# Entering the feed-forward of a hybrid mLSTM and attention block: first weights by seven products, weight sums by adding loads

## The chip, the cores and the metric

The kernel runs on one core of one Trainium2 chip. The metric is device time in microseconds. The kernel before took 1544.88 us (median of three runs, 1544.74 to 1545.6).

Engines are named as in the profile: PE is TensorE (matrix products), DVE is VectorE, ACT is ScalarE, POOL is GpSimd, SP is the engine that issues most transfers.

## The reference

One layer over 1024 tokens of width 1024, everything in float32. An mLSTM mixer and a sparse-attention mixer give two branches; gated, they are summed to `mixed`. What matters for the change is what follows:

```python
h = h + mixed @ w_out                      # 1024 x 1024
f = rms_norm(h, g_norm_ffn)                # per token
h = h + (silu(f @ w_gate) * (f @ w_up)) @ w_down   # 1024 -> 2816 -> 1024
return rms_norm(h, g_final)
```

## The kernel before, in words

**Numbers.** Each float32 operand is split into a rounded high part and a low part (`split_steps`, L1867: a copy on ScalarE, a subtraction on VectorE). A product of two operands is three matmuls (`mm3`, L353 to L355): high times high, high times low, low times high. The word "product" below stands for 12 matmuls of 128 x 128 by 512: four slices of the inner dimension, three matmuls each.

**Seven products for eight.** The products with `w_out`, with the gate and up weights and with `w_down` use a scheme of Winograd's kind. Operands are cut 2 x 2: inner dimension in two halves of 512, rows in even and odd blocks of 128 tokens, columns in two halves. Instead of eight block products there are seven, of sums of blocks; they are numbered by `q`, 1 to 7. Operand 1 and 2 of the rows are the two halves of the even rows; 3 to 7 involve the odd rows too.

**w_out.** For every `q` there are four products, one for each pair of row blocks `j` (`wprod`, L2058). Their results are combined (`post`, L2084) in the buffers `xp[r, c, j]` (r: even or odd row block, c: column half). The input `x` is added by a transfer from memory that adds into the buffer (`xadd`, L2078, through `dma_add`, L1874, issued on GpSimd). Weight sums of `w_out` are made by such adding loads too (`wo_add`, L1991, 1 MB each).

**Passage to the feed-forward.** A finished row half is stored and its squares are summed (`stored`, L2147, `square`, L2096). From two halves the norm factor follows (`rstd_steps`, L2100). `rows_f` (L2153) scales the row (`stt`, L2120: for all even and half the odd rows on ScalarE and then GpSimd, else on VectorE), transposes it on TensorE (L2166, four transposes to a tile), and `row0` (L2173) or `row1` (L2181) and `row1_rest` (L2194) split it or its sums into the operands `fsb[q, j]`.

**Feed-forward.** There are 22 weights `m`: even `m` are gate blocks, odd `m` up blocks, of 256 columns each. The first two, `m` = 0 and 1, are multiplied plainly (`plain_ops`, L2201, `plain`, L2211): four result blocks, two halves of the inner dimension, so eight products each, the four blocks of the even rows first; for the odd rows an extra operand `q` = 8 is made. The other 20 weights go by seven products in the order 1, 2, 6, 7, 5, 4, 3 (`seq`). `load_raw` (L2251) loads a weight in two 512 KB pieces. `sums` (L2259) makes four weight sums: one by a load and an adding load, three on VectorE. `prep` (L2286) splits an operand into one of six operand slots (`OSLOT`), `product` (L2322) multiplies and adds to what was kept, and `finish` (L2302) applies SiLU or multiplies by the gate and stores a tile to `d_gu`.

**The order.** The code lists steps in program order. `Plan` (L66) then places them on the engines by a model of their durations: each engine's queue takes, among the first 60 to 140 steps listed for it (PE: 60), the one that can start first, ties by rank. `pl.boost` raises the rank of the steps listed under it. The result is one fixed order for each engine, GpSimd's and SP's transfers included. A step waits on the chip for what it reads and for its buffer. [...]

Of the kernel before, what the change touches and what calls it, by code (L numbers as in the profile page):

```python
# [9 lines left out]
F32R = mybir.dt.float32r  # L10
# [162 lines left out]
def body(ctx, tc, a, out):  # L173
# [1904 lines left out]
    def xadd(r, c, j):  # L2078
        b = xp[r, c, j]
        i = 2 * j + r  # L2080
        src = a["x"][P * i:P * i + P, 512 * c:512 * c + 512]
        dma_add(lambda: b.ap, lambda: src, [b], 6000.0)
# [70 lines left out]
    def rows_f(r, j):  # L2153
# [27 lines left out]
    def row1(j):  # L2181
        p12, p22 = rows_f(1, j)
        c11, c21 = xp[0, 0, j], xp[0, 1, j]
        at = lambda b: (lambda: four(b.ap))
        t1, t2, t7 = (fpiece((3 * j + n) // 2, (3 * j + n) % 2) for n in range(3)) if j < 2 else (xp[1, 0, j], xp[1, 1, j], fpiece(3, j % 2))
        tsum[j] = {5: t1, 6: t2, 7: t7, 4: c21}
        fsplit(8, j, at(p12), [p12])
        fsplit(3, j, at(p22), [p22])
        act(587.0, lambda: t7.ap, lambda: p12.ap, AF.Copy, [p12], [t7])
        into(V, t1, p12, c11, ALU.subtract, [p12, c11])  # L2190
        into(V, t2, p22, t1, ALU.subtract, [p22, t1])
        into(V, t7, p22, t7, ALU.subtract, [p22])

    def row1_rest(q):  # L2194
        for j in range(4):
            b = tsum[j][q]
            if q == 4:
                into(V, b, b, tsum[j][6], ALU.subtract, [tsum[j][6]])
            fsplit(q, j, lambda b=b: four(b.ap), [b])

    def plain_ops(m):  # L2201
        for kh in range(2):
            b = slot_buf(28 + kh)
            src = a["w_up" if m else "w_gate"].rearrange("(k p) c -> p k c", p=P)
            dma(lambda b=b: rows4(b), lambda kh=kh, src=src: src[:, 4 * kh:4 * kh + 4, 0:256], (), [b])
            for h in range(2):
                o = OB[m, kh, h] = slot_buf(((31, 33, 32, 34), (6, 7, 4, 5))[m][2 * h + kh], F32R)
                src_ = lambda b=b, h=h: rows4(b)[:, :, P * h:P * h + P]
                split_steps(lambda o=o: four(o.ap[:, 0, :]), lambda o=o: four(o.ap[:, 1, :]), src_, [b], [o])

    def plain(m, r, c):  # L2211

        ps = pl.buf()
        fq = ((1, 2), (8, 3))[r]

        for kh in range(2):
            def go(e, kh=kh):
                o, (fh_, fl_) = OB[m, kh, c], blk(fq[kh])
                for k in range(4):
                    mm3(ps.ap, o.ap[:, 0, P * k:P * k + P], o.ap[:, 1, P * k:P * k + P], fh_[:, k], fl_[:, k], kh + k == 0, kh * k == 3)  # L2220
            pl.step((("PE", 12 * 226.7),), go, [OB[m, kh, c]] + [fsb[fq[kh], j] for j in range(4)], [ps])
        if m == 0:
            t = sil[0, (r, c)] = epiece(20 + 2 * c + r)
            act(587.0, lambda: t.ap, lambda: ps.ap, AF.Silu, [ps], [t])
            return
        t, g = epiece(11 + ncount["u"] % 3), sil[0, (r, c)]
        ncount["u"] += 1
        ew(V, lambda: t.ap, lambda: ps.ap, lambda: g.ap, ALU.mult, [ps, g], [t])
        dma(lambda: d_gu[c][:, 512 * r:512 * r + 512], lambda: t.ap, [t], [gub[c]])
# [5 lines left out]
    seq = [(m, q) for m in range(2, NM) for q in (1, 2, 6, 7, 5, 4, 3)]  # L2235
    LO, HI = slice(0, P), slice(P, 2 * P)
    RB, SB_, OB = {}, {}, {}
    EP = (20, 21, 11, 8, 12, 13, 22, 4, 2, 1, 23, 9, 7, 3, 5, 10, 6, 0)

    def epiece(n):  # L2240
        n = EP.index(n)
        return xpiece(n) if n < 16 else piece(60 + n - 16)

    RSLOT = (28, 29, 4, 5)
    OSLOT = (31, 33, 32, 34, 6, 7)
    gub = [pl.buf((), True) for _ in range(NFF)]

    def rows4(b):
        return b.ap.rearrange("p a (k c) -> p (a k) c", k=2)

    def load_raw(n):  # L2251
        m, z = divmod(n, 2)
        if m >= NM:
            return
        b = RB[m, z] = slot_buf(RSLOT[n % 4])
        src = a["w_up" if m % 2 else "w_gate"].rearrange("(k p) c -> p k c", p=P)
        dma(lambda: rows4(b), lambda: src[:, 4 * z:4 * z + 4, 256 * (m // 2):256 * (m // 2) + 256], (), [b], kb=512.0)

    def sums(m, n):  # L2259
        if (m, n) in SB_:  # L2260
            return SB_[m, n]
        r0, r1 = RB[m, 0], RB[m, 1]
        sub = lambda b, h: (lambda: rows4(b)[:, :, h])
        x, y, alu, rd = {1: (sub(r0, HI), sub(r1, HI), ALU.add, [r0, r1]),
                         2: (None, sub(r0, LO), ALU.subtract, [r0]),
                         3: (sub(r0, LO), sub(r0, HI), ALU.subtract, [r0]),
                         4: (sub(r1, LO), None, ALU.subtract, [r1])}[n]
        b = epiece({1: m % 2, 2: 2 + m % 2, 3: 4, 4: 4}[n])
        if n == 1:
            src = a["w_up" if m % 2 else "w_gate"].rearrange("(k p) c -> p k c", p=P)  # L2270
            part = lambda z: src[:, 4 * z:4 * z + 4, 256 * (m // 2) + P:256 * (m // 2) + 2 * P]
            dma(lambda: four(b.ap), lambda: part(0), (), [b])
            dma_add(lambda: four(b.ap), lambda: part(1), [b], 5500.0)
            SB_[m, n] = b
            return b
        if n in (2, 4):
            o = sums(m, n // 2)
            rd = rd + [o]
            x, y = (x or (lambda: four(o.ap))), (y or (lambda: four(o.ap)))
        ew(PREP, lambda: four(b.ap), x, y, alu, rd, [b])  # L2280
        SB_[m, n] = b
        return b

    nop = [0]

    def prep(m, q):  # L2286
        j = nop[0]
        nop[0] += 1
        if q in (1, 2, 4):
            r = RB[m, 0 if q == 1 else 1]  # L2290
            h = HI if q == 4 else LO
            src = lambda: rows4(r)[:, :, h]
        else:
            r = sums(m, {3: 4, 5: 1, 6: 2, 7: 3}[q])
            src = lambda: four(r.ap)
        b = OB[m, q] = slot_buf(OSLOT[j % 6], F32R)
        split_steps(lambda: four(b.ap[:, 0, :]), lambda: four(b.ap[:, 1, :]), src, [r], [b], PREP)

    keep, sil = {}, {}
    ncount = {"u": 0}  # L2300

    def finish(m, blk, ps, other):  # L2302

        s_, w = divmod(m, 2)
        r, c = blk
        if w:
            t = epiece(11 + ncount["u"] % 3)
            ncount["u"] += 1
        else:
            t = epiece(20 + 2 * r + c)  # L2310
# [11 lines left out]
    def product(m, q, part=None):  # L2322
# [11 lines left out]
        if part == 0:  # L2334
            return
# [351 lines left out]
```

## Time and profile before

| | |
|---|---|
| median of three runs | 1544.88 us |
| profiled execution | 1544.09 us |
| its span, first to last instruction | 1542.3 us |
| granted TensorE clock | 0.998 |
| w_out products with group q = 1, from | 809.72 us |
| last eight w_out products, from | 864.65 us |
| even rows of the first two weights | 894.61 to 920.98 us |

Times in a row of the timeline are microseconds from the span's start, then the length. A matmul's bar is longer than the distance to the next, as they are pipelined; the pace is read from starts. In a table of windows each engine has its busy time and number of instructions, then come the clock, the DMA engines' mean busy share and GB/s. A wait row names the waiting engine, what it waited for, total time, times, longest.

### The profile page before, as it was taken

Reading aid. Unit: us, or ns where it says so; the run is one execution under the profiler, and the core shown is the slowest. Engines: PE = TensorE matmul, PEld = TensorE weight load, DVE = VectorE, ACT = ScalarE, POOL = GpSimd, SP = SyncE. Lnnn points to the kernel's source line nnn. Section 1 sums busy time; section 2 is a strip of 40 time slices with the busy share of each in tenths; the row PEclk is TensorE's granted clock in tenths of the full one; section 3 lists DMA queues with packets and bytes.
Section 4 is the critical chain, followed back from the end, with each engine's and each line's share of the span. In section 5 each row is a group of like instructions: output and inputs, shape, how many; then the busy total and the mean of one; then the engine's idle time right before and its main releaser. Section 6 shows DMA issues by size and latency. Waiting matters only on the chain.

```text
span 1542.3 us, 22142 instructions
## 1 busy us (share of the span) xinstructions
PE 1507.2 (98%) x7618; PEld 1271.8 (82%) x7618; DVE 1130.6 (73%) x2393; ACT 807.6 (52%) x1715; POOL 225.0 (15%) x297
## 2 busy tenths in 40 slices
PE   6999999999999999999999999999999999999997
PEld 5877888887989889888888778888888888888886
DVE  6978888875988688875666786666666666785795
ACT  5325566652888688876425664333333333454453
POOL 2000000013121312210001420000000000423311
PEclk9999999999999999999999999999999999999999
DMA  8434755589151924129927724444544443998731
GB/s 278 122 76 119 239 163 164 163 235 281 41 121 41 176 51 115 40 48 342 261 92 177 171 75 116 111 110 126 155 114 110 111 111 106 261 288 179 154 94 55
DMA packets 198777, 223.40 MB, mean 145 GB/s; under 512 B 11960, under 2 KB 144470, under 8 KB 198664
## 3 DMA queue, kind: packets, MB, share of 16 engines
q1 hardware_dynamic: 158024, 175.72, 36.7%
q0 software_dynamic: 40352, 45.60, 18.8%
q8 instruction: 60, 0.98, 0.3%
q10 hardware_dynamic: 288, 0.66, 0.1%
q14 instruction: 53, 0.43, 0.1%
HBM read 171.51 MB, written 58.29 MB: 149 GB/s over the span
## 4 chain that ended last, share of the span: by engine, by line
PE 85%; DVE 6%; DMA 6%; ACT 2%; issue 1%; SPq 0%; DVEq 0%; ACTq 0%; POOLq 0%
PE PS L354 16%; PE PS L353 16%; PE PS L355 16%; PE bk L353 5%; PE bk L354 5%; PE bk L355 5%; PE T L1526 4%; PE obank L1548 2%; PE obank L1546 2%; PE d L353 2%; PE d L355 2%; PE d L354 2%; DMA UTL_float<-in_x 1%; DMA d_mg<-S 1%; DMA ra<-in_w_gate 1%
## 5 line engine op out<-in xcount | busy, mean ns | idle before, releaser
L1862 DVE TENSOR_TENSOR UTL_float<-PS,UTL_float 128x512 f32<-128x512 f32 x160 | 107.5, 688 | 85.2 <-PE PS L355 84.1
L1535 DVE TENSOR_TENSOR TL<-T,TH 128x512 fp32r<-128x512 f32 (+1 forms) x184 | 103.3, 582 | 28.7 <-ACT TH L1531 27.8
L1531 ACT ACTIVATE TH<-T 128x512 fp32r<-128x512 f32 (+1 forms) x184 | 90.3, 510 | 26.4 <-PE T L1526 23.1
L354 PE MATMUL PS<-quad_float32r,sl_float32r 128*128 128x512 f32 x216 | 84.0, 389 | 0.0
L353 PE MATMUL bk<-UTH,op 128*128 128x512 f32 x192 | 77.4, 403 | 0.0
L355 PE MATMUL bk<-UTH,op 128*128 128x512 f32 x192 | 75.0, 391 | 0.0
L354 PE MATMUL bk<-UTL,op 128*128 128x512 f32 x192 | 74.9, 390 | 0.0
L353 PE MATMUL PS<-quad_float32r 128*128 128x512 f32 x192 | 74.8, 390 | 0.0
L355 PE MATMUL PS<-quad_float32r 128*128 128x512 f32 x192 | 74.7, 389 | 0.0
L354 PE MATMUL PS<-quad_float32r 128*128 128x512 f32 x192 | 74.7, 389 | 0.0
L354 PE MATMUL PS<-quad_float32r,whi 128*128 128x512 f32 x168 | 65.5, 390 | 0.7 <-DVE quad_float32r L1862 0.7
L354 PE MATMUL PS<-quad_float32r,wh 128*128 128x512 f32 x164 | 63.8, 389 | 0.0
L353 PE MATMUL bk<-T,op 128*128 128x512 f32 x144 | 58.1, 404 | 0.0
L1560 POOL DMA_DIRECT2D d_yn<-os x32 | 31.9, 996 | 174.1 <-DMA d_yn<-os 40.7
L355 PE MATMUL bk<-T,op 128*128 128x512 f32 x144 | 56.3, 391 | 0.0
L354 PE MATMUL bk<-T,op 128*128 128x512 f32 x144 | 56.2, 390 | 0.0
L353 PE MATMUL d<-UTH,whi 128*128 128x512 f32 x128 | 53.0, 414 | 1.9 <-ACT mg L1398 1.7
L355 PE MATMUL d<-UTH,wlo 128*128 128x512 f32 x128 | 50.4, 394 | 0.0
L354 PE MATMUL d<-UTL,whi 128*128 128x512 f32 x128 | 50.3, 393 | 0.0
L353 PE MATMUL PS<-UTH_float32r,sl_float32r 128*128 128x512 f32 x124 | 48.4, 391 | 0.0
L355 PE MATMUL PS<-UTH_float32r,sl_float32r 128*128 128x512 f32 x124 | 48.3, 389 | 0.0
L725 ACT ACTIVATE op<-S 128x512 fp32r<-128x512 f32 x40 | 25.1, 629 | 43.6 <-PE bk L354 35.0
(1463 smaller groups left out, 4919.6 us busy)
## 6 DMA issues: line engine op xcount, KB each, us to landing
rp<-in_w_in SPq DMA_DIRECT2D x22, 512.0 KB, 4.5
d_gu<-UTL_float SPq DMA_DIRECT2D x44, 256.0 KB, 3.3
sl_float<-in_w_up SPq DMA_DIRECT2D x20, 512.0 KB, 3.8
quad_float<-d_mg SPq DMA_DIRECT2D x32, 256.0 KB, 6.5
d_rep<-d_row SPq DMA_DIRECT2D x8, 960.0 KB, 7.4
raw<-in_w_gate SPq DMA_DIRECT2D x11, 512.0 KB, 4.3
ra<-in_w_gate SPq DMA_DIRECT2D x11, 512.0 KB, 4.2
rp<-in_w_in SPq DMA_DIRECT2D x20, 256.0 KB, 5.0
```

What stands on the lines that cost most here:

```text
L353: nc.tensor.matmul(ps, ah, bh, start=first, stop=False)
L354: nc.tensor.matmul(ps, ah, bl, start=False, stop=False)
L355: nc.tensor.matmul(ps, al, bh, start=False, stop=last)
L725: step1("ACT", 525.0, lambda: nc.scalar.activation(h, src(), AF.Copy), [r], [b])
L1526: nc.tensor.transpose(pt[:, z, P * r:P * r + P], e, ident)
L1531: nc.scalar.activation(hl[0][:, 0:m], pt[:, 0:m], AF.Copy)
L1535: nc.vector.tensor_tensor(hl[1][:, 0:m], pt[:, 0:m], cast32(hl[0])[:, 0:m], ALU.subtract)
L1546: nc.tensor.matmul(po, vv, th[:, z, :], start=(st[1] == 0), stop=False)
L1548: nc.tensor.matmul(po, vv, tl[:, z, :], start=False, stop=(st[1] == st[2]))
L1560: low_half.append(lambda: nc.gpsimd.dma_start(dst, half(1), accum_op=ALU.add))
L1862: return pl.step(alts, lambda e: ENG[e].tensor_tensor(out_(), x(), y(), alu), reads, writes, **kw)
```

## The change

1. `m` = 0 and 1 go by seven products like the others. `plain_ops`, `plain` and operand 8 go. The even rows' products 1 and 2 of weights 0 to 3 come first; then weights 0 and 1 take turns in the order 7, 6, 3, 5, 4; then weights 2 and 3 take that order, one after the other; later weights take 1, 2, 7, 6, 3, 5, 4.
2. All weight sums are made by adding loads: four buffers of 256 KB for each weight, one of which (`x`) is loaded, added to, split for product 7, added to, split for 6, added to, split for 3. Signs are settled in `finish` (SiLU with a factor -1, a multiply with -1).
3. Rows are scaled on VectorE alone.
4. In w_out, the sum for `xp[0, 1]` is started as a copy of `xp[1, 1]` during group 5, and its `x` is added then, ahead of the last product; the adds for the odd rows wait until the 1 MB adding load of `w_out` behind group 3 has landed (`reads=[WT[1]]`). A tiny square root on ScalarE is put ahead of group 3's results. The last eight products run in the order 4, 4, row, 7, row, 7, 4, row, 4, row, 7, 7 instead of 7, row, 4 for each `j`.
5. Stored tiles of `d_gu` are tracked by half, and buffers are handed out from lists (`wfree`, `efree`); the list of free buffers of the down projection has another order.

```diff
-    def xadd(r, c, j):
+    def xadd(r, c, j, reads=()):
...
-            stt(lambda b=b: b.ap, lambda b=b: b.ap, i, lambda c=c: gFb.ap[:, c, :], [gFb], [b], r == 0 or j < 2)
+            stt(lambda b=b: b.ap, lambda b=b: b.ap, i, lambda c=c: gFb.ap[:, c, :], [gFb], [b])
...
     def row1(j):
         p12, p22 = rows_f(1, j)
...
-        fsplit(8, j, at(p12), [p12])
-        fsplit(3, j, at(p22), [p22])
-        act(587.0, lambda: t7.ap, lambda: p12.ap, AF.Copy, [p12], [t7])
-        into(V, t1, p12, c11, ALU.subtract, [p12, c11])
-        into(V, t2, p22, t1, ALU.subtract, [p22, t1])
-        into(V, t7, p22, t7, ALU.subtract, [p22])
+        c11, c21, t7, t6 = xp[0, 0, j], xp[0, 1, j], xp[1, 0, j], xp[1, 1, j]
+        tsum[j] = {7: t7, 6: t6, 5: c11, 4: c21}
+        into(V, t7, c11, p12, ALU.subtract, [p12, c11])
+        fsplit(7, j, lambda: four(t7.ap), [t7])
+        stt_neg(lambda: t6.ap, lambda: p22.ap, lambda: t7.ap, [p22, t7], [t6])
+        fsplit(3, j, lambda: four(p22.ap), [p22])
...
-    seq = [(m, q) for m in range(2, NM) for q in (1, 2, 6, 7, 5, 4, 3)]
+    seq = [(m, q) for q in (7, 6, 3, 5, 4) for m in (0, 1)] + [(m, q) for m in (2, 3) for q in (7, 6, 3, 5, 4)]
+    seq += [(m, q) for m in range(4, NM) for q in (1, 2, 7, 6, 3, 5, 4)]
     OSLOT = (31, 33, 32, 34, 6, 7)
...
+    def w_add(m, n, h, kh):
+        b = WA[m, n]
+        dma_add(lambda: four(b.ap), lambda: w_blk(m, h, kh), [b], 5500.0)
+
+    def prep(m, q):
+        t = {1: "y", 2: "b", 7: "x", 6: "x", 5: "y", 3: "x", 4: "d"}[q]
+        s = WA[m, t]
+        b = OB[m, q] = slot_buf(OSLOT[nop[0] % 6], F32R)
+        nop[0] += 1
+        split_steps(lambda: four(b.ap[:, 0, :]), lambda: four(b.ap[:, 1, :]), lambda: four(s.ap), [s], [b], PREP)
+        if q == 1:
+            w_add(m, "y", 1, 0)
+        elif q == 7:
+            w_add(m, "x", 0, 0)
+        elif q == 6:
+            w_add(m, "x", 0, 1)
+        else:
+            wfree.append(s.home)
+        if q == 3:
+            w_load(m, "d", 1, 1)
+        elif q == 2 and m > 3:
+            chain_load(m)
+
+    def chain_load(m):
+        w_load(m, "x", 1, 1)
+        w_add(m, "x", 1, 0)
...
         out_piece(1, 1, j)
         post(1, 1, j, b5[j], (1, 0), 3)
-        xadd(1, 0, j)
+        out_piece(0, 1, j)
+        act(587.0, lambda d=xp[0, 1, j]: d.ap, lambda x=xp[1, 1, j]: x.ap, AF.Copy, [xp[1, 1, j]], [xp[0, 1, j]])
+        xadd(0, 1, j)
     prep_ab(3, 1)
     wo_add(1, 0, 1)
+    for j in range(4):
+        xadd(1, 1, j, [WT[1]])
+        xadd(1, 0, j, [WT[1]])
+    pl.step((("ACT", 1500.0),), lambda e: nc.scalar.activation(warm, eps, AF.Sqrt), [xp[0, 1, 0]], ())
     b3 = bank()
     for j in range(4):
         wprod(3, j, b3[j])
-        out_piece(0, 1, j)
-        post(0, 1, j, b3[j], (1, 1), 2)
-        xadd(0, 1, j)
-        xadd(1, 1, j)
+        post(0, 1, j, b3[j], None, 2)
+        stored(0, 1, j)
...
     pl.boost = 80
-    for m in range(2):
-        for c in range(2):
-            plain(m, 0, c)
+    for m in range(4):
+        product(m, 1)
+        product(m, 2)
+        if m == 0:
+            for q in (1, 2):
+                prep(3, q)
+            for c in range(4):
+                chain_load(c)
     pl.boost = 0
...
     for n, (m, q) in enumerate(seq):
+        if n < 10 and m == 0 and q in (6, 5, 4):
+            row1_rest(q)
         prep(m, q)
         product(m, q)
+        if q == 3 and 3 <= m < NM - 1:
+            first_loads_e(m + 1)
```

More of the change, by code (lines that the diff above doesn't have):

```diff
@@ L2211, in plain @@
[L2211 to L2229, printed above, removed]
@@ L2251, in load_raw @@
-    def load_raw(n):
-        m, z = divmod(n, 2)
-        if m >= NM:
-            return
[L2255 to L2282, printed above, removed]
@@ L2320, in body @@
-    pb = {}
-    def product(m, q, part=None):
-        o = OB[m, q]
-        ps = pb.setdefault((m, q), pl.buf())
-        js = slice(0, 4) if part is None else slice(2 * part, 2 * part + 2)
-        cs = slice(P * js.start, P * js.stop)
+    seq = [(m, q) for q in (7, 6, 3, 5, 4) for m in (0, 1)] + [(m, q) for m in (2, 3) for q in (7, 6, 3, 5, 4)]
+    seq += [(m, q) for m in range(4, NM) for q in (1, 2, 7, 6, 3, 5, 4)]
+    OSLOT = (31, 33, 32, 34, 6, 7)
+    gub = {(t, c): pl.buf((), True) for t in range(NFF) for c in range(2)}
@@ new lines, in body, with wtake, etake, w_blk @@
+    wfree = [(n, z) for n in (28, 29, 4, 5) for z in range(2)]
+    efree = [(n, z) for n in (0, 1, 2, 3, 30) for z in range(2)]
+    WA, OB, nop = {}, {}, [0]
+    def wtake():
+        n, z = wfree.pop(0)
+        b = fpiece(n, z)
+        b.home = (n, z)
+        return b
+    def etake():
+        h = efree.pop(0)
+        b = xpiece(h[1]) if h[0] == "x" else fpiece(*h)
+        b.home = h
+        return b
+    def w_blk(m, h, kh):
+        src = a["w_up" if m % 2 else "w_gate"].rearrange("(k p) c -> p k c", p=P)
+        c0 = 256 * (m // 2) + P * h
+        return src[:, 4 * kh:4 * kh + 4, c0:c0 + P]
@@ new lines, in chain_load, with first_loads_e, finish @@
+    def chain_load(m):
+        w_load(m, "x", 1, 1)
+        w_add(m, "x", 1, 0)
+    def first_loads_e(m):
+        w_load(m, "y", 0, 0)
+        w_load(m, "b", 0, 1)
+    acc, sil = {}, {}
+    def finish(m, b, r, c, flip=False):
+        s_, w = divmod(m, 2)
+        if w == 0:
+            pl.step((("ACT", 520.0),), lambda e: nc.scalar.activation(b.ap, b.ap, AF.Silu, scale=-1.0 if flip else 1.0), (), [b])
+            sil[s_, r, c] = b
+            return
+        g = sil.pop((s_, r, c))
+        if flip:
+            pl.step((("DVE", 670.0),), lambda e: nc.vector.scalar_tensor_tensor(b.ap, b.ap, -1.0, g.ap, ALU.mult, ALU.mult), [g], [b])
+        else:
+            ew(PREP, lambda: b.ap, lambda: b.ap, lambda: g.ap, ALU.mult, [g], [b])
+        dma(lambda: d_gu[2 * s_ + r][:, 512 * c:512 * c + 512], lambda: b.ap, [b], [gub[2 * s_ + r, c]])
+        efree.extend(x.home for x in (g, b) if x.home[0] in ("x", 30))
@@ L2329, in go, with product @@
+    def product(m, q):
+        o = OB.pop((m, q))
+        ps = pl.buf()
         def go(e):
@@ L2422, in body @@
     wo_add(0, 1, 0)
-    plain_ops(0)
+    for m in range(2):
+        first_loads_e(m)
+        prep(m, 1)
+        prep(m, 2)
     b6 = bank()
@@ L2440, in body, with p4, p7 @@
         wprod(3, j, b3[j])
[L2441 to L2444 removed]
+        post(0, 1, j, b3[j], None, 2)
+        stored(0, 1, j)
     gFb = pl.buf(keys_of(30), make=lambda: f32(30))
     dma(lambda: flat(gFb.ap), lambda: a["g_norm_ffn"].partition_broadcast(P), (), [gFb], kb=512.0)
+    prep_ab(4, 0)
     prep_ab(7, 1)
[L2448 to L2455 removed]
+    b4, b7 = {}, {}
+    def p4(j):
+        b4[j] = pl.buf()
+        wprod(4, j, b4[j])
+        post(1, 0, j, b4[j])
+    def p7(j):
+        b7[j] = pl.buf()
+        wprod(7, j, b7[j])
+        post(1, 1, j, b7[j], None, 2)
+        post(1, 0, j, b7[j])
         stored(1, 1, j)
[L2457 to L2460 removed]
         stored(1, 0, j)
[L2462 removed]
+    p4(0)
+    p4(1)
+    row0(0)
+    p7(0)
+    row0(1)
+    p7(1)
+    p4(2)
+    row0(2)
+    p4(3)
+    row0(3)
+    p7(2)
+    p7(3)
+    for m in (2, 3):
+        first_loads_e(m)
+    for q in (1, 2):
+        prep(2, q)
     for j in range(4):
```

136 lines of the change are left out of this document (35 added, 101 removed).

## The prediction, on record before the run

> **What bounds the kernel now.** I read the page first, then the waits of TensorE, then its timeline around the change, then tables of windows by stage.
>
> ```profile
> span 1542.3 us, 22142 instructions
> PE 1507.2 (98%) x7618; PEld 1271.8 (82%) x7618; DVE 1130.6 (73%) x2393; ACT 807.6 (52%) x1715; POOL 225.0 (15%) x297
> ```
> TensorE is busy for 98% of the span, so a change pays either by taking matmuls away or by filling the few holes. The profiled execution took 1544.09 us (1.8 us around its span); the median of the three runs is 1544.88. My sum is made on 1544.09 and then moved up by that 0.79.
>
> ```profile
> 798.84 0.39 PE L353 MATMUL PS<-sl_float32r,wh 128*128 128x512 f32 x1
> ...
> 801.56 0.39 PE L353 MATMUL PS<-sl_float32r,wh 128*128 128x512 f32 x1
> ...
> 880.80 0.39 PE L353 MATMUL PS<-quad_float32r 128*128 128x512 f32 x1
> 881.49 0.60 PE L2166 MATMUL PS<-cst,UTL_float 128*128 128x128 f32 x4
> ...
> 882.62 0.40 PE L353 MATMUL PS<-sl_float32r,sl_float32r 128*128 128x512 f32 x1
> ```
> The bars overlap, so the pace is read from starts: twelve matmuls lie between the first two rows, 2.72 us, or 0.2267 us each; a "product" (12 matmuls) is 2.72 us. From 880.80 to 882.62 lie six matmuls (1.36 us) and one group of four transposes, which so costs 0.46 us.
>
> ```profile
> 875.53:920.98 45.45, 41.40 (x209) 33.59 (x208) 37.10 (x71) 35.23 (x74) 14.87 (x12) 1.00 0.29 98
> ```
> ```profile
> L2166 PE MATMUL PS<-cst,UTL_float 128*128 128x128 f32 x64 | 9.0, 276 | 2.2 <-POOL UTL_float L1862 2.2
> ```
> ```profile
> PE PS L2166 <- POOL UTL_float L1862: 2.2, 3, 1.2
> PE PS L353 <- ACT UTH_float32r L1865: 1.1, 1, 1.1
> PE PS L354 <- DVE quad_float32r L1862: 0.7, 1, 0.7
> ```
> This window runs from the first transpose to the end of the even rows' plain products. The columns after the length are PE, weight loads, DVE, ACT, POOL, clock, DMA share, GB/s. In it lie the last four w_out products and eight of the feed-forward: 12 x 2.72 = 32.64 us, and 64 transposes: 16 x 0.46 = 7.36. That makes 40.0 of 45.45: **the passage loses 5.45 us**. The waits say to whom: transposes that wait for the rows scaled on GpSimd, then matmuls that wait for the first splits of the transposed rows.
>
> ```profile
> 935.00:1290.00 355.00, 355.00 (x1568) 293.92 (x1567) 227.29 (x355) 115.96 (x189) 23.07 (x18) 1.00 0.46 120
> 1290.00:1320.00 30.00, 30.00 (x134) 24.86 (x133) 19.22 (x31) 14.25 (x24) 4.38 (x5) 1.00 0.49 137
> 1320.00:1440.00 120.00, 120.00 (x531) 99.38 (x530) 82.60 (x133) 54.37 (x94) 33.68 (x39) 1.00 0.91 227
> ```
> After the passage TensorE has no hole at all, with VectorE at 64% (227.29 of 355). What the change takes off VectorE there gains nothing; what it puts on the DMA path could only lose.
>
> **The change part by part.**
>
> *Products.* Before, the first two weights take 4 blocks x 2 halves each, 16 products together; after, 7 each, 14. Two products fewer is 24 x 0.2267 = **-5.44 us**, all on the engine that sets the end. The 28 products of w_out, the 64 transposes and 140 products of the other 20 weights stay.
>
> *Passage, even rows.* The chain is: last add of x, square, norm, scaling, transpose, split.
>
> ```profile
> 851.22 0.86 POOL L1875 DMA_DIRECT2D UTL_float<-in_x  x1 [15.63 <-DVE UTL_float L2039]
> 852.06 1.34 POOL L1875 DMA_DIRECT2D quad_float<-in_w_out  x1
> ...
> 861.43 1.75 POOL L1875 DMA_DIRECT2D UTL_float<-in_x  x2 [0.66 <-DVE UTL_float L1862]
> ```
> ```profile
> 861.91 1.68 ACT L1865 ACTIVATE quad_float32r<-quad_float 128x512 fp32r<-128x512 f32 x3 [5.23 <-DMA quad_float<-in_w_out]
> ```
> ```profile
> 867.09 0.63 ACT L2097 ACTIVATE sq<-UTL_float 128x512 bf16<-128x512 f32 x1 [2.99 <-DMA UTL_float<-in_x]
> ```
> Between 851.22 and 867.09 the 1 MB add of w_out and some five adds of 256 KB land one behind the other: about 2.36 MB in 15.9 us, 1.8 us for each 256 KB. The first square of an even row's right half waits for such an add until 867.09. After the change these four adds are issued a product group earlier, with only the 1 MB add among them; the copy that starts them costs ScalarE four times some 0.63 us (the square's row), off the path. By 1.8 us each from 852 the four and the 1 MB land by about 868 (the second by 864 to 865), and the second row pair is normed near 870.
>
> ```profile
> 864.65 0.39 PE L353 MATMUL PS<-sl_float32r,sl_float32r 128*128 128x512 f32 x1
> ```
> TensorE begins the last eight w_out products at 864.65, and will spend the time to 870.1 on the first two of group 4, so the first transposes no longer stand in line for adds. The eight adds of the odd rows now wait on GpSimd for the 1 MB add (861.9 here). Behind them on that queue stand only later weight sums. They then land 1.8 us apart, from about 870 to 882, and the products that need them end from 867.4 to 890.1 (864.65 + 8 x 2.72 + 8 x 0.46), so their posts keep up.
>
> *Row scaling.*
> ```profile
> 872.95 0.73 ACT L2123 ACTIVATE UTL_float<-UTL_float,sml 128x512 f32<-128x512 f32 x1 [1.03 <-DVE sml L2114]
> ```
> ```profile
> 873.76 2.55 POOL L1862 TENSOR_TENSOR UTL_float<-UTL_float,ra 128x512 f32<-128x512 f32 x2 [5.45 <-ACT UTL_float L2123]
> ```
> ```profile
> 903.45 0.75 DVE L2127 SCALAR_TENSOR_TENSOR UTL_float<-UTL_float,sml,ra 128x512 f32<-128x512 f32 x1
> ```
> Twelve of 16 tiles go from ScalarE plus GpSimd (0.73 + 1.28 us, with GpSimd one at a time) to VectorE, 0.75 each. This takes the wait of 2.2 us away and adds 12 x 0.75 = 9 us to VectorE.
>
> ```profile
> 872.35 0.17 DVE L2112 TENSOR_TENSOR sml<-sml 128x2 f32<-128x2 f32 x1
> ...
> 888.63 1.21 DVE L2112 TENSOR_TENSOR sml<-sml 128x2 f32<-128x2 f32 x1
> ```
> The tiny norm step takes 0.17 us with GpSimd in transfers and 1.21 while GpSimd scales rows. By these rows alone I'd count nothing for it, as two rows prove no cause. [...]
>
> *VectorE in the passage.*
> ```profile
> 864.65:943.00 78.35, 74.30 (x355) 60.78 (x354) 56.71 (x108) 48.71 (x99) 20.92 (x18) 1.00 0.42 109
> ```
> ```profile
> 882.06 1.88 DVE L1862 TENSOR_TENSOR quad_float32r<-PS,UTH_float32r 128x512 fp32r<-128x512 f32 x3
> ```
> From the code, for the two w_out groups, the row work and the first two weights, before: 12 posts, 4 scalings, 8 + 40 steps of the row operands, 4 splits and 4 multiplies: 72 large instructions. After: 12 posts, 16 scalings, 8 + 36 steps, 10 splits, 18 evictions: 100. Beside them come about 7 for the even rows of weights two and three. At 0.61 us each in a row (three take 1.88 with the last one's tail) 28 more are 17 us: 56.7 + 17 = 74 us of VectorE in about 78. It fits, but nearly full. The odd rows' first product (7 of weight 0) starts after 8 products of w_out, 8 even ones and 64 transposes, at about 864.65 + 50.9 = 915.5; its last operand needs the last w_out product (890.1), posts, squares, norm, scaling, transpose, split: about 12 us of chain, 903. So 12 us of even products cover it. The operands of products 5 and 4 are due at 932 and 937, and there a full VectorE can be a few us late. Bounds of what the passage loses after: 0, and 5.45 as before. I take 2.0, nearer to none because each chain named has cover: **-3.45 us**.
>
> *Weight sums by adding loads.* Each weight goes from three VectorE sums and one add to four adds, beside four plain loads and on average two stores of 256 KB. Three of the sums hang on one buffer: the operand of product 7, then an add, 6, an add, 3.
> ```profile
> L1875 POOL DMA_DIRECT2D ra<-in_w_gate x9: 1273/1282/1292, 952.0 to 1249.7; - x9
> ...
> DMA to landing us min/median/max: 4.5/5.3/10.1
> ```
> ```profile
> 969.96 0.63 ACT L1865 ACTIVATE wl<-ra 128x512 fp32r<-128x512 f32 x1 [2.09 <-PE PS L354]
> 972.69 0.63 ACT L1865 ACTIVATE sl_float32r<-UTL_float 128x512 fp32r<-128x512 f32 x1 [2.10 <-PE PS L354]
> ```
> ```profile
> 978.30 0.69 DVE L1862 TENSOR_TENSOR UTL_float<-PS,UTL_float 128x512 f32<-128x512 f32 x1 [0.23 <-PE PS L355]
> ```
> Operand splits start as TensorE frees one of six operand slots, one each product (969.96, 972.69), so five products ahead: 13.6 us before use. Product 3 stands two places after 7, so from the start of 7's split to the use of 3's operand are 19.04 us. Three splits take 3.9 (0.63 + 0.69 each), six hand-overs 1.4 (0.23 each): 13.7 us remain for two adds. At 5.3 each (issue to landing) they take 10.6; there is no wait. The longest, 10.1, with a median one is 15.4, 1.7 too late. Taking it that this happens at most once or twice in the 20 weights, bounds 0 to 3.4, I put in **+1.0 us**. GpSimd's issue goes to 4 x 1.28 = 5.1 of 19 us.
>
> The other edits I cost at nothing: finer tracking of the stored gate-up tiles and the order of free buffers feed the down projection, whose start has TensorE full (30.00 of 30); were its first loads late, each us would count.
>
> **Sum.** 1544.09 - 5.44 - 3.45 + 1.0 = 1536.2; on the median, + 0.79: **1537.0 us**.
>
> **The rivals.**
> *A. The passage loses as much as before*, because VectorE (74 of 78 us) is the bound there and products 5 and 4 wait for their operands. For it: the window's sum. Against: TensorE has other rows' work, and ScalarE's part shrinks. Time: 1544.88 - 5.44 + 1.0 = 1540.4. If it loses 5 more than before: 1545.4, no change.
>
> *B. The chain of adds takes the place of the VectorE sums, and the kernel is slower.*
> ```profile
> q1 hardware_dynamic: 36761, 37.75, 35.0%
> q0 software_dynamic: 9504, 4.72, 10.8%
> ```
> ```profile
> DMA to landing us min/median/max: 4.0/8.5/16.5
> ```
> The first two rows are of 935 to 1290, the third is GpSimd's adds from 1320 to 1440, where the share is 0.91. Of 355 us, 10.8% over 18 adds is 2.13 us of all DMA engines per add; 35.0% over 37.75 MB is 0.86 per plain 256 KB. After: 6 x 0.86 + 4 x 2.13 = 13.7 of 19.04 us, a share of 0.72 against 0.46. On a straight line between 5.3 at 0.46 and 8.5 at 0.91 an add would take 7.15 us; two are 14.3, 0.6 over 13.7, in 20 weights 12 us, in place of my +1.0: 1548. It decides from 6.85 us per add on, and from about 7.05 the gain is gone. Against it: the adds of 1320 to 1440 are issued in bursts and stand behind each other; those of a chain follow one another. [...]
>
> *C. The plan reorders something else* (the planner lists all steps anew), a hole of some us elsewhere: about 1542 to 1546.
>
> **How the numbers follow.** The forecast has 0.58, A 0.18, A with more lost 0.05, B 0.13, C 0.06. The best case is 5.44 + 5.45 gained, 1534.0; with the runs' spread I start the range at 1533.6. Up to 1545.0 it holds the forecast, A, and part of C; B is left out. A measurement tells about 0.2%, 3.1 us, from no change: faster below 1541.8, slower above 1548.0. Faster: nearly all of the forecast and A, 0.75. Same: A with more lost, most of C and the mild half of B, 0.14. Slower: 0.11.
>
> **What would show it.** Right: 24 matmuls fewer on TensorE; the 2.2 us wait of transposes for GpSimd gone; the first square of the even rows' right half before 865; no TensorE wait in the later weights; adds near 5 to 6 us to landing. Wrong: TensorE waiting for splits of products 6 or 3 in every weight, with adds over 6.85 us (B); TensorE waiting for row operands near 915 to 940 with VectorE unbroken (A); a TensorE busy time that is not about 5 us lower.

## The result and the profile after

| | before | after |
|---|---|---|
| median | 1544.88 us (five runs, 1542.57 to 1545.6) | 1536.56 us (five runs, 1535.91 to 1538.33) |
| profiled execution | 1544.09 us | 1537.23 us |
| its span | 1542.3 us | 1535.1 us |
| granted clock | 0.998 | 0.997 |

The ratio of after to before is 0.995, interval 0.9935 to 0.9964: faster by 8.3 us, where 7.9 was forecast. The sum is close. Its terms are not, and the experiments were spent on them. Two executions that ran at a mean granted clock of 0.754, 1891.65 us of the kernel before and 1885.18 us of the version with a product put ahead, are left out of every median and ratio below.

The head of the page of the changed kernel (busy time, share of the span, instructions):

```profile
span 1535.1 us, 22254 instructions
PE 1502.6 (98%) x7594; PEld 1268.6 (83%) x7594; DVE 1107.9 (72%) x2361; ACT 811.1 (53%) x1732; POOL 297.3 (19%) x353
```

TensorE has exactly 24 matmuls fewer (7594 for 7618) and is busy 4.6 us less. To see where the other microseconds lie I took two marks that both kernels have, the first product of w_out's group 1 and the first product of the down projection, from TensorE's timeline. Before:

```profile
809.72 0.39 PE L353 MATMUL PS<-UTL 128*128 128x512 f32 x1
...
1323.54 0.39 PE L353 MATMUL PS<-quad_float32r 128*128 128x512 f32 x1
```

After:

```profile
809.02 0.39 PE L353 MATMUL PS<-UTL 128*128 128x512 f32 x1
...
1316.30 0.39 PE L353 MATMUL PS<-quad_float32r 128*128 128x512 f32 x1
```

The stage between the marks takes 513.82 us before and 507.28 after: 6.54 us less. The last part, down projection included, takes 218.76 and 218.80 to the end of the span: no change. Ahead of the first mark, where TensorE's work is the same, the two executions differ by 0.70; over all profiled executions of the experiments that mark lies between 807.69 and 811.05, so this is spread. In the stage stand 184 products and the transposes before, 184 x 2.72 + 7.36 = 507.84 us of work, so 6.0 are lost; after, 182 products are 502.40 of work, and 4.9 are lost. **The change in the stage is 5.44 from products and 1.1 from the passage**, not 5.44 and 3.45. Below, "lost" is always the stage's length less this work, in one profiled execution.

The windows of the stretches shown for before (PE, weight loads, DVE, ACT, POOL, clock, DMA share, GB/s):

```profile
864.65:943.00 78.35, 76.58 (x360) 63.19 (x361) 74.03 (x143) 48.25 (x96) 12.95 (x11) 0.98 0.64 139
935.00:1290.00 355.00, 355.00 (x1567) 293.92 (x1566) 200.30 (x309) 122.07 (x210) 95.20 (x74) 1.00 0.74 145
1290.00:1320.00 30.00, 30.00 (x134) 24.85 (x133) 19.47 (x32) 13.82 (x25) 8.66 (x9) 1.00 0.74 199
```

VectorE works 74.03 of the 78.35 us of the passage, the forecast 74. The later weights leave TensorE no hole, before as after, with the DMA engines now at 0.74. TensorE's waits between 780 and 1540 us are three (total, times, longest):

```profile
PE PS L355 <- DVE sl_float32r L1862: 1.8, 1, 1.8
PE PS L354 <- DVE quad_float32r L1862: 0.3, 1, 0.3
PE PS L2166 <- DVE UTL_float L2127: 0.3, 1, 0.3
```

The wait for GpSimd is gone and so are those for the first splits. In their place stands one wait at a spot where before had none, in TensorE's timeline at the second product of group 4:

```profile
863.64 0.39 PE L354 MATMUL PS<-sl_float32r,sl_float32r 128*128 128x512 f32 x1
865.79 0.50 PE L355 MATMUL PS<-sl_float32r,sl_float32r 128*128 128x512 f32 x1 [1.76 <-DVE sl_float32r L1862]
866.13 0.39 PE L353 MATMUL PS<-sl_float32r,sl_float32r 128*128 128x512 f32 x1
...
868.27 0.63 PE L354 MATMUL PS<-sl_float32r,sl_float32r 128*128 128x512 f32 x1
868.70 0.63 PE L355 MATMUL PS<-sl_float32r,sl_float32r 128*128 128x512 f32 x1
...
872.54 0.39 PE L353 MATMUL PS<-quad_float32r 128*128 128x512 f32 x1
```

In the trace of before two starts in a row are 0.23 us apart (0.2267 over twelve). Between the first two rows lie 2.15, so 1.9 are lost. Then between 867 and 870.4 starts are 0.43 apart: the 21 matmuls from 866.13 to 872.54 take 6.41 us instead of 4.76, another 1.65. The windows show the clock:

```profile
866.00:868.00 2.00, 2.00 (x8) 1.59 (x8) 2.00 (x4) 2.00 (x5) 1.54 (x2) 0.78 1.12 203
868.00:870.00 2.00, 2.00 (x7) 1.54 (x6) 2.00 (x5) 1.17 (x4) 0.20 (x1) 0.50 1.11 216
```

The granted clock (third column from the right) falls to 0.50; TensorE counts as busy for all of these 2.00 us, but starts a matmul every 0.43 us and not every 0.23. 1.9 and 1.65 are 3.6 of the 4.9 lost. (Whether the fall of the clock belongs to the wait is taken up with the second experiment below.)

What the wait hangs on is seen in VectorE's timeline:

```profile
858.63 1.29 DVE L1862 TENSOR_TENSOR sl_float32r<-quad_float,sl_float32r 128x512 fp32r<-128x512 f32 x2 [1.19 <-ACT sl_float32r L1865]
864.45 0.69 DVE L1862 TENSOR_TENSOR UTL_float<-UTL_float,PS 128x512 f32<-128x512 f32 x1 [4.52 <-DMA UTL_float<-in_x]
865.05 1.89 DVE L1862 TENSOR_TENSOR sl_float32r<-UTH_float,sl_float32r 128x512 fp32r<-128x512 f32 x3
```

VectorE stands 4.52 us for an `x` add. The instruction that waits is a result of group 3 (`post(0, 1, j, ...)`); the three splits behind it (from `UTH`, `prep_a(4, kk)`) are row operands of group 4, and the first of them is what TensorE waits for. Group 4's weights were split before, the last two in the row of 858.63. The add comes from GpSimd's queue:

```profile
851.31 0.89 POOL L1875 DMA_DIRECT2D UTL_float<-in_x  x1 [8.06 <-ACT UTL_float L1865]
851.92 1.61 POOL L1875 DMA_DIRECT2D quad_float<-in_w_out  x1
852.89 1.57 POOL L1875 DMA_DIRECT2D UTL_float<-in_x  x1
...
856.86 4.41 POOL L1875 DMA_DIRECT2D UTL_float<-in_x  x5 [0.69 <-ACT UTL_float L1865]
862.86 0.86 POOL L1875 DMA_DIRECT2D UTL_float<-in_x  x1 [1.60 <-DMA quad_float<-in_w_out]
```

The add awaited is the third, issued at 852.89, right behind the 1 MB add of `w_out`; it lands 11.5 us later, at 864.4. The first one, ahead of the 1 MB, lands in 3.7.

By the last two rows, point 4 of the change is not what happens on the chip. The odd rows' adds don't wait there for the 1 MB to land: in the row of five stand the last add for the even rows and, in the order of `Plan`, four for the odd rows, all issued by 861.27, while the next row still waits for the 1 MB. That wait comes from something else, as an add stands waiting for the 1 MB without the hold too (866.30 in the version with the odd rows' adds not held); in both it is the eighth add behind the 1 MB. The instruction doesn't read the buffer that `reads=[WT[1]]` names. What the hold does is to set the order: it puts the odd rows' adds behind the even rows' in the queue.

### The profile page after: what moved, and what is told of

The parts are those of the page before. It is cut to its first block, busy times and chain, and to the rows that moved or that the text cites. A ratio compares the mean times of both kernels' runs of the same rounds, so it can differ in the third digit from the quotient of the medians.

```text
span 1535.1 us, 22254 instructions
## 1 busy us (share of the span) xinstructions
PE 1502.6 (98%) x7594; PEld 1268.6 (83%) x7594; DVE 1107.9 (72%) x2361; ACT 811.1 (53%) x1732; POOL 297.3 (19%) x353
## 4 chain that ended last, share of the span: by engine, by line
PE 85%; DVE 6%; DMA 5%; ACT 2%; issue 1%; POOL 0%; SPq 0%; DVEq 0%; POOLq 0%; ACTq 0%
PE PS L354 16%; PE PS L353 16%; PE PS L355 16%; PE bk L353 5%; PE bk L354 5%; PE bk L355 5%; PE T L1526 4%; PE obank L1548 2%; PE obank L1546 2%; PE d L353 2%; PE d L355 2%; PE d L354 2%; DMA ra<-in_w_up 1%; DMA rp<-in_w_in 1%; DMA UTL_float<-in_x 1%
## 5 line engine op out<-in xcount | busy, mean ns | idle before, releaser
L1862 DVE TENSOR_TENSOR UTL_float<-PS,UTL_float 128x512 f32<-128x512 f32 x115 | 78.3, 688 | 73.3 <-PE PS L355 71.0
L354 PE MATMUL PS<-quad_float32r,sl_float32r 128*128 128x512 f32 x200 | 77.8, 389 | 0.0
L1865 ACT ACTIVATE UTL_float<-PS 128x512 f32<-128x512 f32 x54 | 31.6, 598 | 68.9 <-PE PS L355 66.9
L1875 POOL DMA_DIRECT2D sl_float<-in_w_up x28 | 36.5, 1305 | 101.4 <-DVE wh L1862 25.0
```

The source lines that it names most:

```text
L354: nc.tensor.matmul(ps, ah, bl, start=False, stop=False)
L1862: return pl.step(alts, lambda e: ENG[e].tensor_tensor(out_(), x(), y(), alu), reads, writes, **kw)
L1865: return pl.step((("ACT", cost),), lambda e: nc.scalar.activation(out_(), x(), fn), reads, writes, **kw)
L1875: pl.step((("Pool", 1000.0),), lambda e: nc.gpsimd.dma_start(dst(), src(), accum_op=ALU.add), reads, writes, lat=lat, kb=kb, nd=1)
```

## The experiments

The theory after this comparison: the passage falls short because group 4's splits stand on VectorE's queue behind an `x` add that lands behind 1 MB. Rivals: VectorE is full, so that the wait only moves; the halved clock is the loss by itself; the gain comes from the scaling rather than the products. Each ratio is to the kernel before on the same chip.

**Two products more.** Does the path follow the number of products?

```diff
-        pl.step((("PE", 12 * 226.7),), go, [o] + ...
+        for _ in range(2 if m < 2 and q == 7 else 1):
+            pl.step((("PE", 12 * 226.7),), go, [o] + ...
```

Product 7 of the first two weights runs twice, so 184 products stand in the stage again.

> The changed kernel with product 7 of weights 0 and 1 computed twice, so that TensorE has the 24 matmuls again that the change took away; the result is the same. Theory (the two products saved are the main gain, at 0.2267 us a matmul, because TensorE is the bound there): 5.4 us more, 1542. Rival (other work is the bound from 915 to 945, VectorE with its row sums, and the saved products would only have filled its holes): 0 to 2 us more, 1536.6 to 1538.5.

Measured: 1541.81 us, ratio 0.9982 (0.9973 to 0.9991); 5.25 us over the changed kernel (4.9 by the two ratios), the stage 512.14, of which 4.3 lost. Within the spread, the 5.44 of the product term is real and lies on the path.

**Group 4's splits ahead of group 3's results.**

```diff
     pl.step((("ACT", 1500.0),), ... AF.Sqrt ...)
+    prep_ab(4, 0)
     b3 = bank()
...
-    prep_ab(4, 0)
     prep_ab(7, 1)
```

> The splits of w_out group 4 are listed ahead of group 3's results, nothing else is edited. Theory (what the passage still loses comes from VectorE's queue: a result of group 3 stands in it, waits 4.5 us for its add of x, and the last splits of group 4 stand behind it, so TensorE waits 1.8 us and then runs at half its clock for 3.4 us): the wait and the slow stretch go, 1.9 + 1.65 = 3.5 us less than the changed kernel, about 1533. Rival 1 (VectorE is simply full in the passage, and whatever goes first makes something else late): no gain, 1536 to 1538, with a TensorE wait of 1 to 3 us elsewhere between 864 and 945. Rival 2 (the slow stretch is a matter of chance, not of the wait): 1.9 us less, with a granted clock below 1 in the passage all the same.

Measured: 1535.96 us, ratio 0.9943 (0.9929 to 0.9956), lost 2.9. The 1.8 us wait is gone, with nothing edited but the order, so the queue was the cause of that wait. But the median is lower by 0.6 us, not by 3.5, and the two intervals overlap. TensorE's timeline, and VectorE's:

```profile
872.53 0.66 PE L2166 MATMUL PS<-cst,UTL_float 128*128 128x128 f32 x4 [2.52 <-DVE UTL_float L2127]
```
```profile
865.27 0.69 DVE L1862 TENSOR_TENSOR UTL_float<-UTL_float,PS 128x512 f32<-128x512 f32 x1 [1.77 <-DMA UTL_float<-in_x]
```

The same add comes no earlier, and now the first transposes wait 2.5 us for the scaled rows that follow from it. Part of what was lost only moved.

The halved clock is gone too, but this doesn't show that the wait had caused it. In three other versions TensorE waits for the same splits, if not as long, and the clock stays at 1.00 from 864 to 880: the wait is 1.49 us with the scaling back on GpSimd, 1.2 with two more products, 0.9 with the later sums on VectorE. The first of them:

```profile
867.55 0.50 PE L355 MATMUL PS<-sl_float32r,sl_float32r 128*128 128x512 f32 x1 [1.49 <-DVE sl_float32r L1862]
```

They lose 4.5, 4.3 and 4.0, where the changed kernel loses 4.9. So the late splits need not bring the stretch at half clock, and where it stays away less than 1.65 is gained, as other waits then come out: 0.6 us at a transpose in the last two.

**A product put ahead of those transposes** (with the edit before):

```diff
-    row0(0)
     p7(0)
+    row0(0)
```

> The run with early group 4 splits, and the first product of group 7 listed ahead of the first rows' transposes. Theory (in that run TensorE waits 2.5 us for the first scaled row because it is scheduled after two products; group 7's operands are there by about 870, so a product of 2.72 us fits into the wait): no wait of TensorE over 1 us at the first transposes, 2 to 2.5 us less than that run, about 1533.5 (1532.5 to 1535). Rival (group 7's splits come later than that, since the 1 MB add lands at 863 and VectorE is full): the wait moves to group 7's first product, 1 to 3 us, and the time stays at 1535 to 1537.

Measured: 1535.35 us (four runs), ratio 0.9939 (0.9925 to 0.9952), lost 4.0. TensorE's waits:

```profile
PE PS L355 <- DVE sl_float32r L1862: 0.9, 1, 0.9
PE PS L2166 <- DVE UTL_float L2127: 0.6, 1, 0.6
PE PS L354 <- DVE quad_float32r L1862: 0.6, 1, 0.6
```

The 2.5 became 0.6, and two new waits for splits, near 888 and 939 us, took its place. VectorE worked 71.89 of 77 us there. No gain beyond the experiment before it can be told.

**Plain loads of x for the even rows' right half** (with `prep_ab(4, 0)` early): the adding loads become plain loads on SP, and VectorE adds.

```diff
+        dma(... xp[0, 1, j] <- x ..., [xp[1, 0, j]], [xp[0, 1, j]])
...
-        act(..., AF.Copy, [xp[1, 1, j]], [xp[0, 1, j]])
-        xadd(0, 1, j)
+        into(V, xp[0, 1, j], xp[0, 1, j], xp[1, 1, j], ALU.add, [xp[1, 1, j]])
```

> On top of the early group 4 splits: x for the right half of the even rows is brought by four plain loads during group 6 and added on VectorE, in place of the ScalarE copies and four adding loads behind which the 1 MB add stands. Theory (both waits, the one for group 4's splits in the changed kernel and the 2.5 us one of the transposes with early splits, come from the same late adds of x): the results of group 3 no longer wait for a transfer, the transposes' wait falls from 2.5 to under 0.5 us, and the time is 2 to 2.5 us below the run with early splits, about 1533.5 (1532 to 1534.5). Rival (VectorE is full, four more instructions on it cost what the transfers gain): transposes still wait 2 us or more, 1535 to 1537.

Measured: 1537.0 us, ratio 0.9956 (0.9942 to 0.997), lost 3.7. The transposes' wait fell to 0.52, but there are four new ones of about 0.25 at group 3. Windows:

```profile
850.00:855.00 5.00, 4.70 (x21) 3.45 (x19) 5.00 (x10) 4.97 (x10) 1.45 (x3) 1.00 0.60 191
855.00:860.00 5.00, 4.31 (x17) 2.75 (x16) 5.00 (x9) 3.39 (x7) 5.00 (x7) 1.00 0.97 159
```

VectorE is busy 10.00 of 10 us and the rows count 38 matmuls on TensorE where it has room for some 44 (5 / 0.2267 = 22 in each window). The add is no longer late; the engine that adds is.

**The same sums on GpSimd.**

```diff
-        into(V, xp[0, 1, j], xp[0, 1, j], xp[1, 1, j], ALU.add, ...)
+        into((('Pool', 1230.0),), xp[0, 1, j], xp[0, 1, j], xp[1, 1, j], ALU.add, ...)
```

> The run with plain loads of x, but its four sums run on GpSimd in place of VectorE. Theory (in that run the gain went into VectorE: with four more sums it had no idle left from 850 to 860 and fed group 3's splits late, four waits of 0.25 us and a slower pace): VectorE gets some 2.4 us back there, those waits go, about 1 to 1.5 us less than with the sums on VectorE, about 1535.5. [...]

Measured: 1539.3 us, ratio 0.9963 (0.995 to 0.9975), lost 6.6. There is no gain; a loss can't be told, as the ratio with the sums on VectorE, 0.9956, lies inside this interval. Of the 6.6 a part is the clock again: it falls to 0.50 from 875.5 to 879.0, after a wait of 1.76 us at the transposes. GpSimd's third and fourth sum, and VectorE's timeline:

```profile
858.79 2.98 POOL L1862 TENSOR_TENSOR UTL_float<-UTL_float 128x512 f32<-128x512 f32 x2 [1.84 <-DVE UTL_float L2039]
```
```profile
854.94 3.17 DVE L1862 TENSOR_TENSOR quad_float32r<-UTH_float,quad_float32r 128x512 fp32r<-128x512 f32 x3
...
859.23 4.30 DVE L1862 TENSOR_TENSOR sl_float32r<-quad_float,sl_float32r 128x512 fp32r<-128x512 f32 x4
863.45 2.48 DVE L1862 TENSOR_TENSOR sl_float32r<-UTH_float,sl_float32r 128x512 fp32r<-128x512 f32 x4
```

Four subtractions that begin beside these sums take 4.30 us, and the four behind them, once GpSimd is done with its sums, take 2.48. So VectorE was relieved of four sums in this run, and what stayed on it took longer beside GpSimd's, by 1.82 us for four.

**The x add ahead of the 1 MB add.** The 1 MB add is listed as a reader of the second `x` add's buffer:

```diff
-    def wo_add(n, kh, ch):
+    def wo_add(n, kh, ch, reads=()):
...
-    wo_add(1, 0, 1)
+    wo_add(1, 0, 1, [xp[0, 1, 1]])
```

> The changed kernel with the 1 MB adding load of w_out made to wait until the add of x for the second even row block has landed. Theory (the adds of one queue land in the order of their issue, and the second x add takes 11.5 us because it stands behind the 1 MB): the second x add lands in 4 to 6 us, near 858; TensorE's 1.8 us wait for group 4's splits shrinks to under 0.5, and the time falls by 2 to 3.5 us, to 1533 to 1535, unless the 1 MB, then landing 5 us or so later (near 867), makes group 7's operands late: then TensorE waits 1 to 3 us for those near 871 and the time is 1535 to 1537. Rival (the adds share the transfer engines evenly, and order does not count): the x add lands in 8 us or more and nothing changes.

Measured: 1540.93 us, ratio 0.9979 (0.997 to 0.9988), lost 9.2. This too is an order and no wait, as GpSimd's timeline shows:

```profile
856.06 0.86 POOL L1875 DMA_DIRECT2D UTL_float<-in_x  x1 [0.70 <-ACT UTL_float L1865]
856.68 1.58 POOL L1875 DMA_DIRECT2D quad_float<-in_w_out  x1
857.44 7.07 POOL L1875 DMA_DIRECT2D UTL_float<-in_x  x7
```

The 1 MB goes out right behind all four adds for the even rows, and seven for the odd rows right behind it. The second `x` add landed 5.5 us after issue, as the theory of the order has it. The time went the other way by 4.4 us:

```profile
870.89 1.41 DVE L2127 SCALAR_TENSOR_TENSOR UTL_float<-UTL_float,sml,ra 128x512 f32<-128x512 f32 x2 [3.78 <-DMA d_h<-UTL_float]
```
```profile
880.17 2.82 PE L2166 MATMUL PS<-cst,UTL_float 128*128 128x128 f32 x12 [2.33 <-DVE UTL_float L2127]
```

Rows are scaled in place, so scaling waits until the row has been stored to memory, and VectorE's queue stands 3.78 us for the store. A split is then 1.4 late too, and the clock falls twice: to 0.50 from 880 to 882, behind the transposes' wait, and again from 921, behind the split's, where starts are 0.43 us apart. Which transfers kept the store back was not tried.

**The odd rows' adds not held.** The change lists eight `x` adds for the odd rows as readers of the 1 MB add's buffer; here they are listed without it.

```diff
-        xadd(1, 1, j, [WT[1]])
-        xadd(1, 0, j, [WT[1]])
+        xadd(1, 1, j)
+        xadd(1, 0, j)
```

> The changed kernel with the odd rows' adds of x no longer held until the 1 MB adding load has landed. Theory (adds of one queue land in the order of their issue, and the odd rows' adds are issued behind the 1 MB and the even rows' adds in any case, as their buffers are ready later): the same within 1 us, 1536 to 1537.5. Rival (they get ahead of even rows' adds, as buffers of group 5 are ready first): the results of group 3 wait longer than 4.5 us in VectorE's queue, TensorE waits 3 us or more for group 4's splits, 1538 or more.

Measured: 1544.52 us, ratio 1.0 (0.9991 to 1.0009), lost 12.1: the whole gain is gone. GpSimd's timeline, VectorE's and TensorE's:

```profile
852.50 1.59 POOL L1875 DMA_DIRECT2D quad_float<-in_w_out  x1
853.26 7.08 POOL L1875 DMA_DIRECT2D UTL_float<-in_x  x7
```
```profile
868.42 0.69 DVE L1862 TENSOR_TENSOR UTL_float<-UTL_float,PS 128x512 f32<-128x512 f32 x1 [7.92 <-DMA UTL_float<-in_x]
```
```profile
869.76 0.80 PE L355 MATMUL PS<-sl_float32r,sl_float32r 128*128 128x512 f32 x1 [5.37 <-DVE sl_float32r L1862]
```

The rival came true: by the order of `Plan`, one odd rows' add now goes ahead of the first even rows' add, and five stand among the seven behind the 1 MB, one of them ahead of the add that VectorE waits for. The even rows' add lands 4 us later, VectorE stands 7.92 us for it, TensorE 5.37 for the splits behind it, and the clock is about half from 868 to 875 (0.53, 0.50, 0.50 and 0.76 in the windows of 2 us from 868 on). It is the wait of the changed kernel, three times as long: the same queue, the same instruction at its head. So what the hold is worth, it is worth by the order alone. Most of the 4 us is the 1 MB itself, which lands some 3.4 us later than in the changed kernel (the add that waits for it goes at 866.30 instead of 862.86); why was not tried.

**Scaling back on GpSimd**, in the changed kernel:

```diff
-            stt(..., [gFb], [b])
+            stt(..., [gFb], [b], r == 0 or j < 2)
```

> The changed kernel with the row scaling as it was: ScalarE and then GpSimd for all even rows and half of the odd ones. Theory (the waits of transposes for GpSimd come from this scaling): 1 to 3 us more than the changed kernel, 1538 to 1540, with waits of TensorE at L2166 for GpSimd, and the tiny norm steps on VectorE stretched above 0.5 us while GpSimd scales. Rival (VectorE's fullness costs more than GpSimd's slowness): 1 to 3 us less, about 1534 to 1536.

Measured: 1536.79 us, ratio 0.9952 (0.9939 to 0.9966), lost 4.5. No difference to the changed kernel; the 1 to 3 us of the theory and those of the rival both stayed away. The tiny norm steps stay at 0.17 us or less from 865 to 910; whether GpSimd scaled beside any of them was not shown. A wait for GpSimd is there again, 0.7 us, and VectorE's busy time between 864.65 and 943 is 68.67 instead of 74.03.

**Scaling on VectorE alone**, in the kernel before:

```diff
-            stt(..., [gFb], [b], r == 0 or j < 2)
+            stt(..., [gFb], [b])
```

> The kernel before with one part of the change alone: all rows scaled on VectorE. Theory (the waits of transposes for GpSimd, 2.2 us in the trace of before, come from the scaling there): 1 to 2.5 us less than before, 1542 to 1543.5, with no wait of TensorE for GpSimd and the tiny norm steps at 0.17 us. Rival (the row chain is late for another reason, the adds of x, so the wait only changes its name, as putting the scaling back into the changed kernel cost nothing): 1544 to 1546, with a wait at L2166 for VectorE instead.

Measured: 1540.8 us, ratio 0.9975 (0.9966 to 0.9984); lost 2.6 of 510.39. TensorE's waits:

```profile
PE PS L2166 <- ACT UTH_float32r L1865: 0.8, 1, 0.8
PE PS L2166 <- DVE UTL_float L2127: 0.7, 1, 0.7
```

By the ratio this one line gives 3.9 us (2.5 to 5.2) in the kernel before, and undone in the changed one it costs nothing that can be told.

**Fewer operand slots.** This puts the chain of adds to the test: with five slots, splits come a product later and there is less room for the adds; with four still less.

```diff
-        b = OB[m, q] = slot_buf(OSLOT[nop[0] % 6], F32R)
+        b = OB[m, q] = slot_buf(OSLOT[nop[0] % 6 if m < 4 else nop[0] % 5], F32R)
```

> The changed kernel with five operand slots in place of six from weight 4 on (18 weights). By the prediction's working the two adds between product 7's and product 3's splits have 13.7 us of room with six slots, so 11.0 with five, and at 4.8 to 5.0 us each they need 9.7: no wait, 1536 to 1538. If adds cost more in the chain than the median says (rival B's case, 5.5 us or more), 0.5 us or more in each of 18 weights: over 1545.

> The same with four slots: room 8.3 us against 9.7 needed, so the chain of adding loads becomes the bound: 1.4 us in each of 18 weights, 25 us more, about 1562 (1552 to 1572), with TensorE waiting for the splits of products 6 or 3. If the sums by adding loads have room to spare that the working does not see: below 1545.

One execution each: 1569.02 us with five, 1539.12 with four (`% 4`). Windows of the later weights, of the changed kernel:

```profile
945.00:1310.00 365.00, 365.00 (x1612) 302.22 (x1611) 200.44 (x308) 125.06 (x216) 96.89 (x76) 1.00 0.75 149
```

with five slots:

```profile
945.00:1310.00 365.00, 352.04 (x1506) 281.00 (x1505) 180.49 (x287) 114.36 (x196) 91.77 (x72) 1.00 0.69 135
```

and with four:

```profile
945.00:1310.00 365.00, 365.00 (x1612) 302.41 (x1611) 200.17 (x311) 128.82 (x217) 98.75 (x77) 1.00 0.75 147
```

With five the time is far outside what was expected; with four the alternative (below 1545) came out, but not by room that the working had missed. There is no wait, since the planner has put product 3 two places further back (1, 2, 7, 6, 5, 4, 3). In the changed kernel too the order on the chip is 1, 2, 7, 6, 5, 3, 4 and not the listed 7, 6, 3, 5, 4. With five slots the planner mixed two weights' products (7, 4, 1, 6, 2, 3, 5 over and over), and TensorE mostly waits for splits on ScalarE (11.0 of 13.1 us of waits from 945 to 1310). That run doesn't measure the chain's room, and why this order costs some 30 us stays open.

**Sums on VectorE again, for the later weights.**

```diff
         b = WA[m, n]
+        if m > 3:
+            t = wtake()
+            dma(... t <- w_blk(m, h, kh) ...)
+            into(V, b, b, t, ALU.add, [t])
+            wfree.append(t.home)
+            return
         dma_add(...)
```

> The changed kernel with the sums of weights 4 to 21 made by plain loads and VectorE additions in place of adding loads: four more VectorE instructions and four plain loads for four adding loads in each of 18 weights. Theory (in the later weights TensorE has no hole with either, so where the sums are made is worth nothing there): the same within 1 us, 1536 to 1537.5, TensorE full from 945 to 1310, DMA share near 0.5 in place of 0.74, VectorE near 70% in place of 55%. Rival (the load on the DMA engines, 0.74, costs the changed kernel time at the start of the down projection or in late landings): 1 to 3 us less, 1533.5 to 1535.5.

Measured: 1536.11 us, ratio 0.9943 (0.9925 to 0.9961), the same as the changed kernel. The windows:

```profile
945.00:1310.00 365.00, 365.00 (x1612) 302.35 (x1611) 246.31 (x384) 132.54 (x221) 5.59 (x5) 1.00 0.51 150
```

VectorE works 46 us more, GpSimd 91 less, the DMA share is 0.51 for 0.75, and TensorE is full in both. Where sums are made in the later weights doesn't matter to the time. (From weight 4 on the planner keeps the listed order 7, 6, 3, 5, 4 in this version.)

## Why the prediction was right, and where it wasn't

**Products: right.** -5.44 forecast, and 5.25 came back when two products were put in (4.9 by the ratios).

**Passage: the term that was mis-sized.** -3.45 forecast ("I take 2.0, nearer to none because each chain named has cover"), -1.1 in the profiled executions, and -1.7 and -2.0 if the two versions with the same passage and no fall of the clock stand for it (two more products, later sums on VectorE). Which of the edits to the passage gave it, other than the scaling, was not tried one by one. The working had the landing right ("the second by 864 to 865"; it was 864.4), but followed that add only to the norm of the second row pair, where TensorE has cover. The chain it didn't name starts at the same add: VectorE takes its work in a fixed order, and behind the result that waits for `x` stood group 4's splits, which TensorE needs from 863.9. The question asked was who uses the add; that of who stands behind its user was not put. The move of `prep_ab(4, 0)` shows that it was the queue. The same holds for the order of the odd rows' adds. The prediction took the hold for a wait on GpSimd and let it pass without a price ("their posts keep up"); it is an order of the queue, and worth 8 us. The 1.8 us for each 256 KB was too long as well: from 864.4 to 869.7 five adds behind the 1 MB land some 1.3 us apart.

Rival A named the other half. VectorE works 74 of 78 us there, and three repairs (the early splits, a product ahead, plain loads) each removed or cut their wait and gave no more than can be told from the spread: another wait for VectorE followed. That VectorE's fullness is the reason is shown with plain loads (10.00 of 10 us) and argued for the other two; with the early splits the late add has a part in the new wait. The price of 5.45 was too high; the changed kernel and its three repairs lose 2.9 to 4.9.

**The halved clock** was in no term: 1.65 us of the 4.9 in the profiled execution. Three versions with a shorter wait for the same splits show none, and one with a wait of 2.52 us elsewhere none either; what decides it stays open.

**Scaling: right in kind, wrong as a separate term.** The wait for GpSimd went. Alone it is worth 3.9 us (2.5 to 5.2) in the kernel before, undone nothing that can be told in the changed kernel: it can't be given a share of the 8.3 us. The tiny norm step that took 1.21 us takes 0.16 to 0.17 at all its ten places in the kernel before with this one line changed. But the experiment changed who scales as well, so the price of the overlap by itself was not measured for these steps.

**Adding loads: 0 instead of +1.0.** Landing, from the adds of 1000 to 1280 us:

```profile
DMA to landing us min/median/max: 4.3/4.8/10.2
```

At a share of 0.75 (forecast 0.72) the median fell from 5.3 to 4.8 rather than rising to 7.15: rival B's straight line from a burst of adds to a chain of adds did not hold. And the room was counted on the listed order: on the chip product 3 comes a place later, so 13.7 + 2.7 = 16.4 us were there, more than even 10.2 with a median one. The planner had made the room that the prediction missed.

**Down projection and rival C:** 0, as costed. On the profiled executions the four errors are +2.35 (passage), -1.0 (adds), -0.7 (ahead of the stage) and +0.3 (around the span): 1537.23 for a forecast of 1536.2. They nearly cancel, so that the median came within 0.5 us of the forecast is luck; that it came out some 8 us lower is not, as the products alone are 5.4 of it. The best versions measured (0.9939 and 0.9943) can't be told from the changed kernel (0.995).

## What to carry to other kernels

When a result waits for a transfer, look at what stands behind it on the same engine's queue, not only at who reads the result; order those ahead that need no transfer. Where one engine is full through a passage, as VectorE was here (74.03 of 78.35 us), look for the next wait behind the one that is removed, as three repairs met one; so count that engine's work first and expect a fraction of the wait. What an edit is worth alone is not what it is worth beside others: the scaling gave 3.9 us by itself and nothing that can be told beside the rest. And look on the chip whether a dependency that the plan knows is a wait there too: here it was an order.

## What the hardware showed that was not expected

- In the changed kernel the clock fell to 0.50 for some 3.4 us, beginning 1.3 us after a wait of 1.76 us, and cost 1.65 us. The length of the wait alone doesn't decide it: among the versions the clock fell after waits of 1.42 and 2.33 us (the x add ahead) and 1.76 (sums on GpSimd), and during one of 5.37 (odd rows' adds not held, for some 6.8 us), and not after waits of 0.9, 1.2, 1.49 and 2.52 (early splits). What does decide it no run here shows.
- Adding loads of one queue landed in the order of issue, from 815 to 1310 us in the traces of both kernels (39 adds before, 107 after). 256 KB took 11.5 us behind 1 MB in the changed kernel, 5.5 ahead of it in the version with the x add ahead, and 3.7 with no other add under way.
- In one case, the x add ahead, VectorE stood 3.78 us for the store of a row that is scaled in place.
